# The RWKV-7 core on compact operands: array tiles on the diagonal and 16x16 block inverses

## The chip, the cores and the metric

The kernel runs on one core of a Trainium2 chip. The metric is the device time of one execution in microseconds (us); lower is better. Before the change three timed runs gave 2174.22, 2177.02 and 2177.87 us; the median, 2177.02 us, is the time to predict against. Engines are named as in the profile: PE is TensorE's matmul side, PEld its weight loads, DVE is VectorE, ACT ScalarE, POOL GpSimd, SP the queue that issues the DMAs.

## What is computed

Four layers of a bidirectional sequence model on 256 context and 256 latent tokens of 1024 features, all in fp32: retention, mLSTM, RWKV-7, retention. Only the third layer is touched. Its core is a recurrence over tokens for 16 heads of 64 features in two directions; every head has a state S of 64 x 64:

```
def step(S, inp):
    rt, wt, kt, vt, at, bt = inp
    sa = einsum('bhij,bhj->bhi', S, at)
    S = S * wt[:, :, None, :] + sa[..., None] * bt[:, :, None, :] + vt[..., None] * kt[:, :, None, :]
    return S, einsum('bhij,bhj->bhi', S, rt)
...
mu = y.mean(-1); var = mean(square(y - mu))
o = (y - mu) * rsqrt(var + RWKV_GN_EPS) * gn_g + gn_b
o = (o + bonus) * silu(gate)
```

The scan runs over the context first, then over the latents from the context's last state. `y` is the sum of both directions, normalised head by head.

## The kernel before

Tokens go in 8 chunks of 64 for each direction, heads in 8 pairs (two heads of 64 features fill 128 partitions), pairs in two halves `hf` of four. A unit is one chunk of one direction and one half: four pairs, eight heads. A stage `n` (0 to 7) is four units: two chunks, both directions, one half. Within a chunk the recurrence becomes products: `a`, `r`, `b` and `k` with the decay in them, a strictly triangular 64x64 matrix L of a head, and the inverse of (I - L).

`rk_core` writes the stages out in a fixed order (`ORDER`): `P` (`prep`) loads k, kk and r, makes the decay and the decayed operands; `G` (`grams1`) the products of b with a and r; `H` (`grams2`) those of k; `I` (`solve`) inverts; `J` (`whole`) joins the inverse's parts into M and multiplies the part RB by it to give G; `T` (`step`) of the stage before takes the state one chunk further; `A` is a piece of the last layer's modulation. The framework then orders each engine's queue by its own simulated timeline; every engine works its queue in order.

The operands of both heads of a pair stand block-diagonally in 128x128 tiles, with zeros between (`rb`, `rk`, `rV`, `rR`, `roff`, M, Q, S; zeroed once, then each head's block is written by an operation of its own on 64 partitions). So every product is one full 128-row product for the pair. `bb` (line 1308, VectorE) and `kb` (line 1320, GpSimd) are written that way, S is updated at line 1441, ScalarE copies R (shown as `bdB<-pp`).

`grams1` (line 1330) leaves the 32x32 diagonal blocks of L, 16 pairs in all of a stage, in `AD`, by four copies a unit on ScalarE (`AD<-g`). `solve` masks `AD` (line 1368), transposes it so that a block lies in a partition (line 1369, into `LS`), and eliminates in 30 steps: each is a multiply and an add (lines 1380 and 1381), the first 6 columns on GpSimd in a copy of their own, the rest on VectorE. Lines 1386 and 1387 transpose the result back, as O1 and O2 (`O`). There are two `AD` buffers from the second stage on, and one `LS`. `whole` copies the diagonal blocks of O2 to M (`bdB<-O`, ScalarE), and makes the block below the diagonal with two rounds of products (lines 1398 and 1405); line 1411 gives G. `step` has lines 1426 and 1428 (R), 1435, 1437 and 1438 (the output and the new state in one product of 128 columns). `finish`, once for four steps of a tile, normalises; it takes the square root on ScalarE.

During stage 0, and up to about 1280 us, `rk_rest` runs the projections of r, the values and the gates on TensorE; only then `second()` opens the buffers of the later stages.

Of the kernel before, what the change touches and what calls it, by code (L numbers as in the profile page):

```python
# [7 lines left out]
F32 = mybir.dt.float32  # L8
F32R = mybir.dt.float32r
PSUM = bass.MemoryType.PSUM  # L10
# [19 lines left out]
CS, AKN, GN, WN, RBN, KBN = 8, 8, 4, 4, 5, 2  # L30
ENG = (0, 0, 1, 1, 1, 0, 0, 0)
SC = 6
# [16 lines left out]
class Norm:  # L49
    """The layer's norm of one stream over its features, taken up tile by tile. The sums are of the differences to the  # L50
    mean of the first 128 features, which is within a few standard deviations of the mean."""
# [17 lines left out]
    def add(self, c):  # L69
# [10 lines left out]
        # four partial sums, each on 32 partitions  # L80
# [22 lines left out]
    def finish(self):  # L103
# [16 lines left out]
        # the last layer adds to the latents alone  # L120
# [3 lines left out]
    def late(self):  # L124
        """What the next layer adds to."""
        nc = self.net.nc
        for k in range(KT):
            x = self.x[k]
            nc.gpsimd.tensor_tensor(out=x, in0=x, in1=self.rs, op=OP.mult)
            nc.gpsimd.tensor_scalar(out=x, in0=x, scalar1=self.cs[:, 2, k:k + 1], scalar2=self.cs[:, 3, k:k + 1], op0=OP.mult, op1=OP.add)  # L130


class Net:
# [41 lines left out]
    def filler(self, n=0):  # L175
        """The next piece of what the layer can do at any time."""
# [8 lines left out]
    def open_pw(self, name, bufs=(3, 4, 4), side="right"):  # L185
        """Weights: raw and in their exact parts, on the other side of SBUF."""
# [8 lines left out]
    def open_slots(self, es, name, groups, side="left"):  # L195
        """Slots by what they are for: the tiles of a group take theirs in turn."""
# [3 lines left out]
    def t(self, name, dt=F32, n=512):  # L200
        """A slot of at most 512 columns."""
# [4 lines left out]
    def q(self, name, n=HALF):  # L206
        """A small slot of at most 256 columns."""
# [13 lines left out]
    def pt(self, tag, n=512):  # L221
        """A bank of PSUM."""
# [21 lines left out]
    def unit(self, w, n0, n=256, lo=0, hi=None):  # L244
        """Columns n0.. of w in their exact parts, a pair of [128, n] for each 128 rows."""
# [14 lines left out]
    def proj(self, w, c, lo, hi):  # L260
        """Feature-major product of 128 columns with the tokens lo..hi."""
# [6 lines left out]
    def first_proj(self, jobs, by_k=False, po=4):  # L268
        """proj for a layer's first jobs (w, c, lo): the context's tokens ahead of the latents', or the input's features in turn."""
# [16 lines left out]
    def halves(self, src, h, l, eng=None):  # L286
        """src into its exact parts."""
# [38 lines left out]
    def make_h(self, i, k, st, src, s, b):  # L326
        """h = src * s + b, the input of layer i, in its exact parts (whole for the RWKV layer)."""
# [41 lines left out]
    def out_rows(self, i, w, r0, z, lo0, streams, units=None):  # L369
        """x += gate * (z @ w[r0:r0+512]); z in 4 pairs of tiles of 128 features, from token lo0."""  # L370
# [31 lines left out]
    def log_sigmoid_(self, x, tl):  # L402
        """-(max(-x, 0) + log1p(exp(-|x|))), the logarithm by its atanh series."""
# [22 lines left out]
    def columns(self, ps, parts):  # L426
        """Sums over the partitions of tiles; parts: the columns of 128 of ps that a tile of 128 queries adds to."""
# [3 lines left out]
    def rows(self, col, n, tag="ps"):  # L431
        """Columns of 128 back to n values along the free dimension, the same in every partition."""
# [7 lines left out]
    def rsqrt_rows(self, squares, n, scale, eps, tag="ps"):  # L440
        """(scale * sums over the partitions + eps) ** -0.5 for n columns."""
# [9 lines left out]
    # ---------------------------------------------------------------- retention  # L451
# [37 lines left out]
    def ret_masks(self, h, w384, lg, lgx):  # L489
        """exp(distance * log gamma) summed over the directions, by (query - key): within a stream, latents to context."""  # L490
# [42 lines left out]
    def ret_v(self, h, v, u, w_in):  # L533
        """Half of the values, tokens on partitions."""
# [11 lines left out]
    def ret_values(self, h, qk, v, w_in, w_out, streams, rope, w384, lg, lgx):  # L546
# [4 lines left out]
        # scores of a tile of keys, [keys, queries]  # L551
# [37 lines left out]
        # gates  # L589
# [12 lines left out]
    # ---------------------------------------------------------------- mLSTM  # L602
    def mlstm(self, i, j):
        nc, a = self.nc, self.a
        w_in, w_out = a["ml_w_in"][j], a["ml_w_out"][j]
        with ExitStack() as es:
# [3 lines left out]
            # what goes on into the next layer  # L610
# [12 lines left out]
            def gate_weights(g):  # L623
                """The gates' weights for the convolved and the plain stream, of 4 tiles."""
# [16 lines left out]
            # the convolved stream, that of half the heads by way of memory, and the gates  # L641
# [39 lines left out]
            # the plain stream and the outer gate go by way of memory until their head's turn, as does what the layer adds to  # L681
# [57 lines left out]
    def ml_gates(self, gps, sel, gb, cst):  # L739
        """Rows 32 * direction + head: -G = -max(0, cummax(g)) to memory, g = i - B and exp(-(B + G)) by column."""  # L740
# [76 lines left out]
        # decay of both directions  # L817
# [10 lines left out]
    def ml_scores(self, h, parts, gcol, ecol):  # L828
        """Decayed scores [keys, queries] of both directions and the inverse denominators."""
# [29 lines left out]
        # denominators  # L859
# [29 lines left out]
    def ml_v(self, h, xmd):  # L889
        """Values without their mean over the head, tokens on partitions."""  # L890
# [67 lines left out]
    def spans(jt, d):  # L958
        """The queries that see key tile jt in direction d."""
# [4 lines left out]
    def rwkv(self, i, j):  # L964
        nc, a = self.nc, self.a
        mm = nc.tensor.matmul
        with ExitStack() as es:
# [5 lines left out]
                      ("mrb", (2, 64)), ("mtri", (32,)), ("reset", (512,)))  # L973
# [20 lines left out]
            # by feature, V by token  # L994
# [192 lines left out]
    def rk_core(self, es, e0, K, B, xd, h, xx, p1, p0):  # L1187
# [76 lines left out]
        if ENG[3]:  # L1264
            vcopy = copy
# [417 lines left out]
```

## Time and profile before

| | |
|---|---|
| median of three timed runs | 2177.02 us (2174.22 to 2177.87) |
| profiled execution: span, first to last instruction | 2169.8 us (a time of its own is not listed) |
| TensorE busy | 1958.8 us, 90% |
| VectorE busy | 1351.0 us, 62% |
| ScalarE busy | 942.3 us, 43% |
| GpSimd busy | 614.8 us, 28% |
| core of the RWKV layer | about 1180 to 1760 us of the span |

A busy share is that of the whole span. A product's record covers its way through the array, so that a busy TensorE is not one at its peak. A plain fp32 product stands as two records in the trace, each of them with a weight load. "<-X" in a row means that the time before it ended when X was done.

### The profile page before, as it was taken

To read this page: it belongs to the slowest core of one execution; us is meant where nothing else is said; L and a number is where in the kernel's file an instruction comes from. 1 tells how busy PE (TensorE), PEld (TensorE's weight loads), DVE (VectorE), ACT (ScalarE), POOL (GpSimd) and SP (SyncE) were. 2 spreads that over 40 slices of the span, in tenths; PEclk is the share of its full clock that TensorE was granted. 3 is DMA by queue.
4 is the path that set the end of the run, shared out by engine and by line. 5 is a ranking of instruction groups with operands and counts; after the bars stand their busy time and mean duration, and the time that the engine had idled before them with its cause. 6 is when DMAs were issued, how large, how long until landed. Compare 5 with 4: busy or idle time off the path is not lost.

```text
span 2169.8 us, 35237 instructions
## 1 busy us (share of the span) xinstructions
PE 1958.8 (90%) x13594; PEld 1666.2 (77%) x13594; DVE 1351.0 (62%) x2472; ACT 942.3 (43%) x1853; POOL 614.8 (28%) x940
## 2 busy tenths in 40 slices
PE   6999999998999899987999987778878988999996
PEld 5788888877778777775758976677877776999995
DVE  4463535358536477676857467878877665665554
ACT  3342414134435454333435555555756342444433
POOL 1000000007100334324303266655656332311001
PEclk9999999999999999998899998889889999999998
DMA  9333333333545553441235411111222740233331
GB/s 299 118 98 120 114 112 123 92 107 109 193 155 159 169 175 127 136 155 52 76 132 164 148 57 52 40 28 44 63 60 82 236 148 15 78 113 121 117 98 48
DMA packets 241527, 245.94 MB, mean 113 GB/s; under 512 B 30992, under 2 KB 200080, under 8 KB 241360
## 3 DMA queue, kind: packets, MB, share of 16 engines
q1 hardware_dynamic: 241360, 243.70, 35.6%
q8 instruction: 107, 1.75, 0.3%
q14 instruction: 60, 0.49, 0.1%
HBM read 216.26 MB, written 27.39 MB: 112 GB/s over the span
## 4 chain that ended last, share of the span: by engine, by line
PE 65%; DVE 18%; ACT 5%; DMA 4%; issue 4%; POOL 3%; SPq 0%; DVEq 0%; ACTq 0%; POOLq 0%
PE pp L256 15%; PE pp L257 15%; PE pp L258 15%; DVE LS L1381 2%; DVE sol L1380 2%; PE po L257 2%; PE ps L83 2%; PE po L256 2%; PE po L258 2%; DMA raw<-ada_w 1%; ACT bdB L1200 1%; PE ps L308 1%; DVE wl L240 1%; ACT AD L1200 1%; PE g L1330 1%
## 5 line engine op out<-in xcount | busy, mean ns | idle before, releaser
L240 DVE TENSOR_TENSOR wl<-wraw,wh 128x1024 fp32r<-128x1024 f32 x216 | 270.8, 1255 | 202.9 <-ACT wh L238 195.1
L238 ACT ACTIVATE wh<-wraw 128x1024 fp32r<-128x1024 f32 x216 | 228.6, 1059 | 265.8 <-PE pp L257 111.7
L256 PE MATMUL pp<-hA,wh 128*128 128x512 f32 (+1 forms) x704 | 255.4, 365 | 6.6 <-DVE rp L527 3.0
L257 PE MATMUL pp<-hB,wh 128*128 128x512 f32 (+1 forms) x704 | 254.8, 363 | 0.0
L258 PE MATMUL pp<-hA,wl 128*128 128x512 f32 (+1 forms) x704 | 254.6, 363 | 0.1
L256 PE MATMUL pp<-zh,wh 128*128 128x512 f32 (+1 forms) x620 | 216.0, 351 | 10.6 <-ACT zh L288 6.0
L258 PE MATMUL pp<-zh,wl 128*128 128x512 f32 (+1 forms) x620 | 210.8, 340 | 0.0
L257 PE MATMUL pp<-zl,wh 128*128 128x256 f32 (+1 forms) x512 | 169.2, 330 | 3.1 <-DVE zl L289 3.1
L367 DVE SCALAR_TENSOR_TENSOR x<-pp,mod,x 128x256 f32<-128x256 f32 x192 | 87.3, 480 | 132.8 <-PE pp L258 132.4
L256 PEld LDWEIGHTS pp<-hA,wh 128*128 128x128 f32 x704 | 132.5, 189 | 31.5 <-PE pp L258 3.6
L258 PEld LDWEIGHTS pp<-hA,wl 128*128 128x128 f32 x704 | 133.1, 189 | 23.9 <-issue 1.6
L257 PEld LDWEIGHTS pp<-hB,wh 128*128 128x128 f32 x704 | 133.1, 189 | 22.4 <-issue 1.7
L256 PEld LDWEIGHTS pp<-zh,wh 128*128 128x128 f32 x620 | 117.9, 191 | 40.2 <-issue 10.2
L256 PE MATMUL pp<-wh,hA 128*128 128x256 f32 x512 | 145.7, 286 | 2.0 <-ACT wh L238 1.9
L257 PE MATMUL pp<-wl,hA 128*128 128x256 f32 x512 | 144.9, 284 | 0.8 <-DVE wl L240 0.8
L258 PE MATMUL pp<-wh,hB 128*128 128x256 f32 x512 | 144.5, 283 | 0.0
L258 PEld LDWEIGHTS pp<-zh,wl 128*128 128x128 f32 x620 | 118.3, 191 | 20.2 <-issue 7.6
L1380 POOL TENSOR_TENSOR sol<-AD 128x84 f32<-128x84 f32 (+13 forms) x240 | 97.0, 404 | 117.9 <-ACT AD L1200 100.6
L257 PEld LDWEIGHTS pp<-zl,wh 128*128 128x128 f32 x512 | 98.2, 192 | 16.7 <-issue 5.4
L1381 POOL TENSOR_TENSOR AD<-AD,sol 128x84 f32<-128x84 f32 (+13 forms) x240 | 98.0, 408 | 18.2
L256 PEld LDWEIGHTS pp<-wh,hA 128*128 128x128 f32 x512 | 96.9, 190 | 5.9 <-issue 2.7
L257 PEld LDWEIGHTS pp<-wl,hA 128*128 128x128 f32 x512 | 97.3, 190 | 1.7 <-DVE wl L240 1.0
(519 smaller groups left out, 4911.4 us busy)
## 6 DMA issues: line engine op xcount, KB each, us to landing
wraw<-ret_w_in SPq DMA_DIRECT2D x96, 512.0 KB, 3.7
wraw<-ada_w SPq DMA_DIRECT2D x56, 512.0 KB, 4.0
wraw<-ret_w_out SPq DMA_DIRECT2D x32, 512.0 KB, 3.4
wraw<-ml_w_in SPq DMA_DIRECT2D x32, 512.0 KB, 3.8
wraw<-rk_w_rkvg SPq DMA_DIRECT2D x32, 512.0 KB, 3.6
adaw<-ada_w SPq DMA_DIRECT2D x48, 256.0 KB, 4.5
raw<-ada_w SPq DMA_DIRECT2D x16, 512.0 KB, 7.6
wraw<-ml_w_out SPq DMA_DIRECT2D x16, 512.0 KB, 4.7
```

Of the source, the lines that this page charges most:

```text
L83: nc.tensor.matmul(self.sums[32 * j:32 * j + 32, n * HALF:n * HALF + HALF], net.ones[:, 0:32], src, start=c < 4 and n == 0, stop=c >= 4 an ...
L238: nc.scalar.activation(h, t, ACT.Copy)
L240: (nc.gpsimd if self.nsplit % 4 in self.psplit else nc.vector).tensor_tensor(out=l, in0=t, in1=f(h), op=OP.subtract)
L256: mm(ps, lhs[0], rhs[0], start=start, stop=False)
L257: mm(ps, lhs[0], rhs[1], start=False, stop=False)
L258: mm(ps, lhs[1], rhs[0], start=False, stop=stop)
L308: nc.tensor.matmul(ps[32 * j:32 * j + 32, 0:m].rearrange("p (b q) -> p b q", b=nb), self.csil[:, k, :], raws[k // n][:, k % n, j], start=k ...
L367: self.nc.vector.scalar_tensor_tensor(out=x, in0=ps, scalar=self.gate(i, c, st), in1=x, op0=OP.mult, op1=OP.add)
L1200: copy = lambda o, x: nc.scalar.activation(o, x, ACT.Copy)
L1330: mm(g[:, p, 0:192], cat(u["bb"][:, p]), W[:, p], start=True, stop=True)
L1380: eng.tensor_tensor(out=t, in0=A[:, s + 1:, s:s + 1].broadcast_to([128, m, n]), in1=A[:, s:s + 1, lo:hi].broadcast_to([128, m, n]), op=OP. ...
L1381: eng.tensor_tensor(out=A[:, s + 1:, lo:hi], in0=A[:, s + 1:, lo:hi], in1=t, op=OP.add)
```

## The change

Operands become compact: the two heads of a pair stand one above the other (`[128, 4, 64]` instead of `[128, 4, 2, 64]`), and each head's product is an own small product placed on the array by `tile_position`. A head's 64 rows go to the tile at (0, 0) or (64, 64); the first gram uses four tiles of 64 rows and 32 columns; the products of the inverse's parts use four 32x32 tiles on the diagonal, or two at (0, 32) and (64, 96). Zeroing the buffers falls away but for M and `AD`. `step` makes three sums in PSUM banks of their own (R, the output, the new state) instead of two.

`solve` inverts two 16x16 blocks of each 32x32 block side by side, in 14 steps on VectorE alone; GpSimd has no part in it. The block between them (`Lo`, masked out of the same product) is joined in `whole` by three more rounds of 64 small products each (64, 64 and 64) before the two rounds that were there. The masks go into `grams1` as two VectorE operations a unit.

Other edits: `ENG` moves the `+ 1` of the decay (line 1295) and the bonus product of `finish` (line 1493) from VectorE to GpSimd; R is copied out of PSUM by one ScalarE operation instead of two; the decay of a chunk's end (`Dc`) is one copy instead of two; rings of `b`, `k`, `V` and `R` have four buffers instead of two, M has two; `finish` takes its root with GpSimd's power instead of ScalarE's Sqrt, and loads the values in four DMAs instead of one. Comments and docstrings are emptied, which the cut leaves out.

```diff
-CS, AKN, GN, WN, RBN, KBN = 8, 8, 4, 4, 5, 2
-ENG = (0, 0, 1, 1, 1, 0, 0, 0)
-SC = 6
+CS, AKN, GN, WN, RBN = 8, 8, 4, 4, 5
+ENG = (1, 0, 1, 1, 1, 0, 0, 1)
...
+        pa = self.ph.tile([128, 8, 2, 4, 64], F32, tag="A", name="bdA")
+        pb = self.ph.tile([128, 16, 4, 64], F32, tag="B", name="bdB")
+        rb, rk = [Ring([pa[:, m] for m in ms]) for ms in (range(4), range(4, 8))]
+        rV, rR = [Ring([pb[:, m] for m in ms]) for ms in (range(4), range(4, 8))]
+        rM = Ring([pb[:, m:m + 4].rearrange("p u q t -> p (u q) t") for m in (8, 12)], zero)
...
-            for h in range(2):
-                r = slice(64 * h, 64 * h + 64)
-                E_B.tensor_tensor(out=bb[r, :, :, h].rearrange("p s q t -> p q s t"), in0=st(rev(kk))[r], in1=st(em)[r], op=OP.mult)
+            E_B.tensor_tensor(out=bb.rearrange("p s q t -> p q s t"), in0=st(rev(kk)), in1=st(em), op=OP.mult)
...
         def grams1(u, b0, AD):
             for p in range(4):
-                mm(g[:, p, 0:192], cat(u["bb"][:, p]), W[:, p], start=True, stop=True)
+                for h, r in heads:
+                    for half in range(2):
+                        q = 64 * h + 32 * half
+                        for o, c in (((0, 192), (0, 192)),) if half == 0 else (((0, 32), (32, 64)), ((64, 192), (64, 192))):
+                            mm(g[q:q + 32, p, o[0]:o[1]], bb[r, p, 32 * half:32 * half + 32], W[r, p, c[0]:c[1]], start=True, stop=True,
+                               tile_position=(64 * h, q))
+            for n, t in ((0, AD[:, :, b0:b0 + 4]), (1, u["Lo"])):
+                nc.vector.tensor_tensor(out=t, in0=g[:, :, 0:32].rearrange("p q t -> p t q"), in1=K["m16"][:, n].unsqueeze(2).broadcast_to([128, 32, 4]), op=OP.mult)
-            for q in range(4):
-                r, half = slice(32 * q, 32 * q + 32), q % 2
-                (vcopy if half else copy)(AD[r, :, b0:b0 + 4].rearrange("p t q -> p q t"), g[r, :, 32 * half:32 * half + 32])
...
         def solve(n, AD):
+            for s in range(1, 15):
+                m = 15 - s
+                t = p0.tile([128, 112], F32, tag="sol", bufs=1, name="sol")[:, 0:2 * m * s].rearrange("p (k a b) -> p k a b", k=2, b=s)
+                nc.vector.tensor_tensor(out=t, in0=A[:, :, s + 1:16, s:s + 1].broadcast_to([128, 2, m, s]), in1=A[:, :, s:s + 1, 0:s].broadcast_to([128, 2, m, s]), op=OP.mult)
+                nc.vector.tensor_tensor(out=A[:, :, s + 1:16, 0:s], in0=A[:, :, s + 1:16, 0:s], in1=t, op=OP.add)
...
         def whole(units, O1, O2):
+            for b in range(16):
+                for o, r in quarters:
+                    mm(ps[r, b], units[b // 4]["Lo"][r, :, b % 4], O2[r, :, b], start=True, stop=True, tile_position=(o, o))
+            nc.vector.tensor_tensor(out=Pm, in0=ps, in1=K["m16"][:, 2].unsqueeze(1).broadcast_to([128, 16, 32]), op=OP.add)
+            ...
+                    mm(ps[r, b], O1[r, :, b], Pm[r, b], start=True, stop=True, tile_position=(o, o))
+            for q, (o, r) in enumerate(quarters):
+                (gcopy if q % 2 else copy)(M[r, :, 32 * (q % 2):32 * (q % 2) + 32], ps[r])
+            ...
+                    mm(ps[r, b], Pm[r, b], O1[r, :, b], start=True, stop=True, tile_position=(o, o))
+            copy(MT, ps)
+            ...
+                    mm(ps[r2, b], units[b // 4]["off"][r, b % 4], M[r, b, 0:32], start=True, stop=True, tile_position=(o, o2))
+            for h, (o, r, o2, r2) in enumerate(low):
+                (gcopy if h else copy)(Q[r2], ps[r2])
+            ...
+                    mm(ps[r2, b], MT[r2, b], Q[r2, b], start=True, stop=True, tile_position=(o2, o2))
+            for h, (o, r, o2, r2) in enumerate(low):
+                (gcopy if h else copy)(M[r2, :, 0:32], ps[r2])
...
         def step(u):
+            def sums(*terms):
+                ps = self.pt("pp", 256).rearrange("p (q f) -> p q f", q=4)
+                for n, (x, c, y) in enumerate(terms):
+                    for p in range(4):
+                        for h, r in heads:
+                            mm(ps[r, p], x[r, p, c:c + 64], y[r, p], start=n == 0 and p == 0, stop=n == len(terms) - 1 and p == 3, tile_position=(64 * h, 64 * h))
+                return ps
+            known = lambda c: [(AK, c, V)] + [(W, c, s0)] * (s > 0)
+            copy(R, sums(*known(0)))
+            y_ = sums(*known(64), (G, 0, R))
+            if s < 7:
+                f_ = sums(*known(128), (G, 64, R))
+                nc.vector.tensor_tensor(out=s0, in0=f_, in1=u["Dc"].unsqueeze(2).broadcast_to([128, 4, 64]), op=OP.mult)
```

## Rows read from the trace of the kernel before

**Rows 1.** The page's span line, and TensorE's busy time, share and instructions.
```profile
span 2169.8 us, 35237 instructions
PE 1958.8 (90%) x13594; PEld 1666.2 (77%) x13594; DVE 1351.0 (62%) x2472; ACT 942.3 (43%) x1853; POOL 614.8 (28%) x940
```

**Rows 2.** Windows: stretch, length, busy time of each engine, granted clock, DMA share, GB/s.
```profile
1240.00:1260.00 20.00, 20.00 (x105) 15.99 (x104) 19.03 (x41) 5.75 (x14) 17.06 (x38) 1.00 0.14 46
...
1306.00:1708.00 402.00, 321.29 (x2653) 289.25 (x2653) 321.32 (x657) 222.89 (x539) 252.78 (x508) 0.89 0.24 68
1269.00:1306.00 37.00, 28.86 (x246) 25.87 (x245) 18.29 (x28) 30.96 (x75) 18.42 (x20) 1.00 0.22 65
```

**Rows 3.** The chain that ended last, 1100 to 1860 us: start, duration, what.
```profile
1306.27 1.25 DVE LS L1369
...
1356.73 1.86 DVE O L1387
...
1416.84 1.87 DVE O L1387
...
1658.40 1.91 DVE O L1387
...
1706.11 1.85 DVE O L1387
```

**Rows 4.** Groups by line, 1306 to 1708 us: count, busy us, mean ns, idle before.
```profile
L1380 POOL TENSOR_TENSOR sol<-AD 128x84 f32<-128x84 f32 (+13 forms) x210 | 85.7, 408 | 97.9 <-ACT AD L1200 82.9
L1381 POOL TENSOR_TENSOR AD<-AD,sol 128x84 f32<-128x84 f32 (+13 forms) x210 | 85.3, 406 | 15.8
L1381 DVE TENSOR_TENSOR LS<-LS,sol 128x24 f32<-128x24 f32 (+7 forms) x168 | 68.3, 406 | 7.7 <-ACT AD L1200 3.7
L1380 DVE TENSOR_TENSOR sol<-LS 128x24 f32<-128x24 f32 (+7 forms) x168 | 66.9, 398 | 4.1
...
L1441 DVE TENSOR_TENSOR S<-pp,Dc 64x256 f32<-64x256 f32 x50 | 21.4, 427 | 1.2
...
L1308 DVE TENSOR_TENSOR bdA<-kk,em 64x512 f32<-64x512 f32 x24 | 18.6, 774 | 0.4
...
L1201 DVE COPY G<-ps 128x512 f32<-128x512 f32 x12 | 8.2, 682 | 1.9 <-PE ps L1411 1.9
...
L1380 DVE TENSOR_TENSOR sol<-LS 128x114 f32<-128x114 f32 x14 | 5.8, 411 | 0.2
...
L1380 DVE TENSOR_TENSOR sol<-LS 128x24 f32<-128x24 f32 x14 | 3.6, 259 | 0.3
...
L1358 DVE TENSOR_TENSOR bon<-bon,g 128x128 f32<-128x128 f32 x8 | 2.2, 271 | 0.1
...
L1200 ACT ACTIVATE AD<-g 32x128 f32<-32x128 f32 x96 | 36.7, 382 | 18.6 <-PE g L1330 17.4
L1200 ACT ACTIVATE bdB<-O 32x512 f32<-32x512 f32 x25 | 27.1, 1085 | 9.1 <-DVE O L1387 8.7
```

**Rows 5.** Timeline, TensorE: start, duration, line, output<-inputs, weights, moving operand, count.
```profile
1295.26 1.95 PE L1411 MATMUL ps<-RB,bdB 128*128 128x128 f32 x16
...
1312.14 0.43 PE L1353 MATMUL g<-th,hrk 128*32 128x128 f32 x8
1312.50 1.57 PE L1346 MATMUL g<-W,bdA 128*128 128x192 f32 x8
...
1274.08 2.06 PE L1398 MATMUL ps<-O,q 128*64 128x32 f32 x32
...
1283.98 2.05 PE L1405 MATMUL ps<-Q,AD 128*32 128x64 f32 x32
...
1317.13 0.27 PE L1287 MATMUL g<-tw,cw 64*128 64x128 f32 x1
1317.14 0.27 PE L1287 MATMUL g<-ta,ca 64*128 64x128 f32 x1
1317.24 0.27 PE L1287 MATMUL g<-tw,cw 64*128 64x128 f32 x1
```

More of the change, by code (lines that the diff above doesn't have):

```diff
@@ L1254, in rk_core @@
         rAK = Ring([p1.tile([128, 4, 192], F32, tag="AK", bufs=4, name="AK") for _ in range(4)])
-        S = {}
+        S, lo = {}, [None]
+        heads = [(h, slice(64 * h, 64 * h + 64)) for h in range(2)]
         Y, bon = {}, {}
@@ L1385, in solve @@
+            nc.vector.memset(flat[:, ::33], 1.0)
             O1 = AD
-            nc.vector.transpose(fl(O1), fl(LS))
-            nc.vector.transpose(O2, LS.rearrange("p t s -> p s t"))
+            nc.vector.transpose(fl(O1), flat)
+            nc.vector.transpose(O2, flat.rearrange("p (t s) -> p s t", t=32))
             return O1, O2
         def whole(units, O1, O2):
-            for q in range(4):
-                r, half = slice(32 * q, 32 * q + 32), q % 2
-                (vcopy if half else copy)(M[r, :, q // 2, 32 * half:32 * half + 32], O2[r, :, 0:16].rearrange("p t q -> p q t"))
@@ L1395, in whole @@
[L1395 to L1407 removed]
+            quarters = [(32 * q, slice(32 * q, 32 * q + 32)) for q in range(4)]
@@ new lines, in whole @@
+            copy(MT, ps)
+            ps, Q = wide(), part("Q")
+            low = [(64 * h, slice(64 * h, 64 * h + 32), 64 * h + 32, slice(64 * h + 32, 64 * h + 64)) for h in range(2)]
+            for b in range(16):
+                for o, r, o2, r2 in low:
+                    mm(ps[r2, b], units[b // 4]["off"][r, b % 4], M[r, b, 0:32], start=True, stop=True, tile_position=(o, o2))
+            for h, (o, r, o2, r2) in enumerate(low):
+                (gcopy if h else copy)(Q[r2], ps[r2])
+            ps = wide()
@@ L1486, in finish @@
+            for h, r in heads:
+                for x in range(2):
+                    t0 = 128 * j + 64 * x
+                    nc.sync.dma_start(v[r, x], B["V"][t0:t0 + 64].rearrange("s (p h f) -> s p h f", p=8, h=2)[:, P, h])
             nc.sync.dma_start(sg, B["g"][P, :, tok].rearrange("q p t -> p q t"))
-            bt = bank("ps")[:, 0, 0:8]
-            mm(bt.rearrange("p (q h) -> p q h", h=2), bon[j, hf].rearrange("p s t -> p (s t)"),
-               self.ident.rearrange("p (q c) -> p q c", c=32)[:, :, 0:2], start=True, stop=True)
+            bt = bank("ps")[:, 0, 0:8].rearrange("p (x q) -> p x q", x=2)
@@ L1490, in finish @@
+            for x in range(2):
+                for h, r in heads:
+                    mm(bt[r, x], bon[j, hf][:, x], self.ident.rearrange("p (q c) -> p c q", c=32)[:, h], start=True, stop=True, tile_position=(0, 64 * h))
             bc = tl("bc", 2, 8)
-            copy(bc, bt)
-            v3 = v.rearrange("p q (h j) -> p (q h) j", h=2)
-            E_V.tensor_tensor(out=v3, in0=v3, in1=b3(bc), op=OP.mult)
+            copy(bc.rearrange("p (x q) -> p x q", x=2), bt)
+            E_V.tensor_tensor(out=flat(v), in0=flat(v), in1=b3(bc), op=OP.mult)
@@ L1494, in finish @@
             o, bn = bank("ps"), bank("ps")
-            for p in range(4):
-                mm(o[:, p], Y[j, hf][:, p], self.ident, start=True, stop=True)
-            for p in range(4):
-                mm(bn[:, p], v[:, p], self.ident, start=True, stop=True)
+            for out, src in ((o, Y[j, hf]), (bn, v)):
+                for p in range(4):
+                    for x in range(2):
+                        for h, r in heads:
+                            mm(out[r, p, 64 * x:64 * x + 64], src[r, x, p], K["II"][r], start=True, stop=True, tile_position=(64 * h, 64 * h))
```

138 lines of the change are left out of this document (49 added, 89 removed).

## The prediction

> **What bounds the kernel now.** I read the page first: TensorE is busy for 90% of a span of 2169.8 us [rows 1]. That is an average over four layers, and the change touches only the core of the third, so I went to the windows next. There the core splits in two. Up to about 1280 us the other projections of the layer run on TensorE beside the first stage, and TensorE is busy without a gap (20.00 of 20.00 us in the window from 1240) [rows 2]: what becomes shorter beside it there is hidden. From 1306 to 1708 us no engine is full: of 402 us TensorE is busy for 321, VectorE for 321, GpSimd for 253, ScalarE for 223, and TensorE's granted clock is 0.89 of 2.4 GHz on average, so that it spent part of this stretch at its lower level of 1.2 GHz [rows 2].
>
> The chain of waits tells what sets the pace there. A stage's inversion opens with the transpose at L1369 and closes with the one at L1387. The closings lie at 1356.73, 1416.84 and, later, 1658.40 and 1706.11 us, some 50 to 60 us apart, and the second stage opens at 1306.27 [rows 3]. Seven stages, the second to the eighth, take 1306.3 to 1708.0 us: 57.4 us each. LS, the buffer that is inverted, is one buffer, so inversions follow one another, and one takes nearly a whole period: 30 steps, each two operations on VectorE and two on GpSimd, with all other VectorE work of the stage queued in between. In the groups of lines of these 402 us L1380 and L1381 alone are 135.2 us on VectorE (19.3 a stage) and 171.0 us on GpSimd (24.4 a stage) [rows 4]. So the bound is a serial chain on VectorE and GpSimd, and TensorE waits inside it.
>
> **The change part by part**, a stage at a time (four units, each one chunk of four pairs of heads).
>
> Inversion: 30 steps on 32x32 become 14 steps on two 16x16 blocks at once, 28 operations of 28 to 112 elements, on VectorE alone. Such an operation now takes 259 ns at 24 elements and 411 ns at 114, with GpSimd working beside it [rows 4]. That bounds the 28 at 7.3 and 11.5 us; I take 8.5, nearer to the low end, because GpSimd is out of the step and half of the sizes are under 90. VectorE loses 19.3 and gains 8.5 us; GpSimd loses 24.4 and gains nothing here. The serial piece with its three transposes (4.4 us) becomes about 13 us, a quarter of the period, so it no longer sets the pace.
>
> Masking and copies: ScalarE's copies into AD, 96 of 382 ns in the stretch (up to 16 a stage, 6.1 us), give way to two masked VectorE operations of 128 elements a unit. The nearest row is L1358, 128 elements from PSUM in 271 ns: 8 x 0.27 = 2.2 us. The four copies of O into M, 1085 ns each, leave ScalarE (4.3 us) [rows 4].
>
> Joining on TensorE evicts ten pieces of 512 columns: one sum, four parts of M, MT, two of Q, two of M again; six smaller old copies go. Priced by the 128x512 copy from PSUM at 682 ns [rows 4], VectorE gets five (3.4 us), ScalarE about as much.
>
> Compact operands: the pairs of half-height operations at L1308 (774 ns) and L1441 (427 ns) become one operation of full height, and time goes by columns: two of 774 and 3.5 of 427 ns go from VectorE, 3.0 us [rows 4]. Masking, sums over Y, the step moved to GpSimd (E_L, E_V) and the small old copies take about another 3 us off it; GpSimd has 24 us of new room for that. VectorE, busy for 321 / 7 = 45.9 us a stage now [rows 2], goes to 45.9 - 19.3 + 8.5 + 2.2 + 3.4 - 3.0 - 3 = 35 us. ScalarE and GpSimd fall well below.
>
> TensorE: a product of fp32 is two instructions in the trace. Sixteen of 128 columns (L1411) take 1.95 us, so that they start some 0.11 us apart (the last one lasts 0.3); eight of 192 columns (L1346) 0.16 us apart; of the small ones, 32 with 64 weight columns and 32 moving ones (L1398) take 2.06 us, 32 with 32 and 64 (L1405) 2.05, both some 0.057 to 0.062 apart [rows 5]. Now: 4 units x 40 x 0.11 = 17.6 us in the steps, 5.1 for each kind of gram, 7.4 in joining (2.0 + 1.9 + 3.5), 4.5 for the rest: 39.7. After: tiles on the diagonal go in pairs or fours. That neighbours on different tiles run together is shown: the lora products of L1287 on two row tiles start 10 ns apart, the next pair 0.11 us later, as one product alone would, and the eight of L1353 on four column tiles fit into 0.43 us [rows 5]. Then a step is 32 pairs of two instructions at 0.057 to 0.062: 3.7 to 4.0 us, a stage 14.6 to 16. The first gram, in four 64x32 tiles, keeps the 192 columns of its longest tile and some waits in order: 5.7; the second stays 5.1. Joining has five rounds of 16 blocks, two instructions each at 0.031 (32 columns at half the pace of L1405's 64, or at L1398's) to 0.062: 5 to 10 us, and the last product stays 3.5. With the rest 38 to 45, I take 41.5.
>
> The unknown in joining is how closely small instructions follow. The pairs of L1287 start 10 ns apart, but averaged over a run no row shows less than some 0.05 us an instruction (eight in 0.43 us) [rows 5]. The Trainium skill ("TensorE: Matmul & The Clock Gate", "Wait — 56ns, not 53.3ns?") states that start-to-start never drops below some 25 ns; by that joining's 512 small instructions would take 12.8 us and the stage's TensorE work about 48 us. The 10 ns of L1287's pairs speak against it as a hard floor.
>
> TensorE's busy time now is 321 / 7 = 45.9 us a stage against the 39.7 of dense work; the 6.2 between are fills, waits in a group and the low clock [rows 2]. With the same 6.2 the new stage is 47.7 on TensorE, above VectorE's 35.
>
> **Sum.** The period goes from 57.4 to about 48 us: 7 x 9.4 = 66 us. Before it, in 1269 to 1306, where ScalarE is busy 31 of 37 us [rows 2], 16 AD copies (6.1 us) go: 6 us, from bounds of 0 and 8. After it, the last steps lose 3 us on TensorE (17.6 to 14.6), and joining's longer chain of dependent rounds (five for two, each with an eviction) takes the place of the 4.3 us of O copies: 3 us, from bounds of -3 and 6. Together 75 us. On the span that is 2169.8 - 75 = 2095; the three timed runs have a median of 2177.0, so 7.2 us lie around the span, and the forecast is 2102.
>
> **The rivals.**
> First, TensorE packs better than I allow: its work is 38 us, VectorE's 35, and the stages pipeline with few fills. The period is then 42: 7 x 15.4 + 12 = 120 us, about 2057. For it: TensorE ran at the low clock mainly because it waited for the inversion. Against: two engines at nine tenths, each in order and each feeding the other, seldom come that close.
>
> Second, the dependent rounds and the change of tile shape between groups cost more. Some 35 groups a stage would each start behind the drained previous one; L1353's eight end at 1312.57, so the last began about 1312.30, and the next kind of product begins at 1312.50 [rows 5]: 0.2 us where 0.11 is usual, 0.09 lost. At 0.2 us a group and 12 us of small instructions the stage is 54: 7 x 3.4 + 5 = 29 us, about 2148. The Trainium skill ("TensorEngine Tiling (Array Packing)", "Key Properties") says that changing the mode drains the engine, which agrees with the 0.09.
>
> Third, on the other side: diagonal tiles don't run together. By the code the two row tiles of L1287 write different banks of PSUM, and the column tiles of L1353 share all rows; no row shows two row tiles that write one bank, which is what every product of the change does. If they take turns, the steps are 29 to 32 us a stage, the grams 10 each, joining 23 to 39, the rest 6: at least 80, period 85 to 95, 7 x 33 = 230 us more: about 2400. It decides from the point where serial tiles bring a stage above 57.4 us. "TensorEngine Tiling (Array Packing)", "Gotcha 1: PSUM Pressure", in the Trainium skill says that different row tiles cannot access the same PSUM bank at once; read strictly, that is this rival. For the diagonal, output partitions differ too, as they do in L1353's column tiles, which overlap in one bank; so I hold it unlikely.
>
> Fourth, the change does not bear: TensorE's order, PSUM's two banks for each kind, and GN's four buffers keep the period at 57. About 2175.
>
> **How the numbers follow.** Forecast (period 45 to 52) 0.60; first rival 0.16; second 0.12; third 0.08; fourth 0.04. Faster by over 0.2% (4.4 us, about what a measurement of this kernel can tell from no change) is 0.60 + 0.16 + 0.12 = 0.88, within 0.2% 0.03, slower 0.09. The range is 2045 to 2150: from a little under the first rival to the second.
>
> **What would show it.** Right: inversions of some 13 us with gaps between them, L1387's counterparts 45 to 52 us apart; TensorE busy over 90% of the stretch; pairs on the diagonal starting within 10 ns. Wrong: a pair whose second product starts only when the first is through (third rival); four-tile rounds of 16 blocks over 2.5 us (second); VectorE, not TensorE, full in the windows; or the time from 1280 to 1306 grown by a wait for the first stage.

## The result, and the profile after

The changed kernel takes 2276.62 us (median of 4, 2266.20 to 2279.48) against 2177.03 us before: ratio 1.045, 95% interval 1.0425 to 1.0475. Faster by 75 us was forecast; it is slower by 100 us. The page of after, to be read against [rows 1]:

```profile
span 2277.7 us, 50954 instructions
PE 2031.2 (89%) x21898; PEld 1712.7 (75%) x21898; DVE 1241.5 (55%) x2316; ACT 840.1 (37%) x1653; POOL 424.7 (19%) x432
```

VectorE, ScalarE and GpSimd lost 110, 102 and 190 us of work as intended, and TensorE gained 72 us. In windows (length, busy time of each engine, granted clock, DMA share, GB/s) the six stages from the second to the eighth inversion's start:

```profile
1322.70:1757.80 435.10, 331.56 (x8569) 295.71 (x8567) 215.64 (x462) 139.59 (x376) 91.02 (x72) 0.78 0.18 49
```

No engine is full, as in [rows 2], but now TensorE runs at 0.78 of 2.4 GHz (0.89 before) and still stands idle for 17 us of each stage of 72.5 us. One stage in the chain of waits (start, duration, what; "issue" is time in which the engine waited for nothing that the profile shows), to be read against [rows 3]:

```profile
1389.21 1.15 DVE LS L1370
...
1400.54 1.81 DVE O L1380
...
1402.40 2.26 PE ps L1392 x125
1404.66 2.11 PE pp L1441 x34
1406.76 1.95 PE ps L1397 x120
...
1411.31 1.47 issue
...
1413.10 1.73 PE ps L1409 x64
...
1418.50 1.84 PE ps L1415 x62
...
1427.70 3.73 PE pp L1441 x126
1431.43 1.75 PE g L1284 x26
...
1434.56 1.50 POOL em L1292
...
1436.08 1.24 DVE em L1293
...
1445.87 1.58 DVE bdA L1302
...
1447.49 4.54 PE g L1327 x63
...
1454.43 1.15 DVE LS L1370
```

The inversion (L1370 to L1380) is down to 13.2 us, as forecast. But the rest now follows it in a row: joining rounds (L1392 to L1415) with steps (L1441) between them, steps, the next stage's preparation (L1284 on TensorE, L1292 on GpSimd, L1293 and L1302 on VectorE), its grams (L1327), and only then the next inversion. Before, nearly all that lay in the long inversion's shadow: the next inversion opened 0.5 to 16 us after one had closed, where it now opens 52 to 70 us after. Two openings of before, to be set beside the closings of 1356.73 and 1416.84 in [rows 3]:

```profile
1360.07 1.23 DVE L1369 STREAM_TRANSPOSE LS<-AD 128x1024 f32<-128x1024 f32 x1
...
1419.18 1.24 DVE L1369 STREAM_TRANSPOSE LS<-AD 128x1024 f32<-128x1024 f32 x1
```

The time that TensorE waits in the kernel after, by what ended the wait (us in total, times, longest), the six stages:

```profile
PE g L1327 <- DVE bdA L1302: 21.5, 10, 3.4
PE pp L1441 <- ACT bdB L1199: 21.2, 6, 5.0
PE ps L1392 <- DVE O L1380: 16.5, 6, 3.1
PE g L1347 <- ACT AK L1199: 11.5, 6, 2.0
PE ps L1403 <- issue: 10.9, 6, 2.2
```

Grams wait for the preparation, steps for R's copy, joining for the inversion, once a stage each (the grams up to twice).

### The profile page after: what moved, and what is told of

Its sections match the earlier page's. It is cut to its first block, busy times and chain, and to the rows that moved or that the text cites. A ratio compares the mean times of both kernels' runs of the same rounds, so it can differ in the third digit from the quotient of the medians.

```text
span 2277.7 us, 50954 instructions
## 1 busy us (share of the span) xinstructions
PE 2031.2 (89%) x21898; PEld 1712.7 (75%) x21898; DVE 1241.5 (55%) x2316; ACT 840.1 (37%) x1653; POOL 424.7 (19%) x432
## 4 chain that ended last, share of the span: by engine, by line
PE 71%; DVE 13%; DMA 5%; issue 4%; ACT 4%; POOL 2%; SPq 1%; ACTq 0%; POOLq 0%; DVEq 0%
PE pp L255 14%; PE pp L256 14%; PE pp L257 14%; PE pp L1441 4%; PE po L256 2%; PE po L255 2%; PE po L257 2%; PE g L1327 2%; PE ps L82 2%; PE ps L1422 2%; DMA raw<-ada_w 1%; PE ps L307 1%; DVE sol L1375 1%; DVE wl L239 1%; DVE LS L1376 1%
## 5 line engine op out<-in xcount | busy, mean ns | idle before, releaser
L257 PEld LDWEIGHTS pp<-wh,hB 128*128 128x128 f32 x512 | 98.0, 191 | 0.0
L1441 PE MATMUL pp<-bdB,AK 64*64 64x64 f32 x1472 | 88.2, 251 | 8.5 <-DVE S L1450 5.2
```

The costliest lines, as they stand in the source:

```text
L257: mm(ps, lhs[1], rhs[0], start=False, stop=stop)
L1441: mm(ps[r, p], x[r, p, c:c + 64], y[r, p], start=n == 0 and p == 0, stop=n == len(terms) - 1 and p == 3, tile_position=(64 * h, 64 * h))
```

## Experiments

Ratios are to the kernel before, timed on the same chip. The table gathers the traces: period is the mean of the six stages above; TensorE's busy share and granted clock are those of the same stages (by windows); the last column is how long after an inversion's start the next stage's first Tanh (the head of its preparation) runs, as a mean of six.

| kernel | us | ratio | period | TensorE busy | clock | next preparation after |
|---|---|---|---|---|---|---|
| before | 2177 | 1 | 61.1 | 0.78 | 0.88 | 17 |
| before_14 | 2104.9 | 0.968 | 51.4 | 0.87 | 0.94 | 15 |
| mix | 2143.6 | 0.984 | 54.5 | 0.94 | 0.96 | 13 |
| old_step | 2156.2 | 0.991 | 57.2 | 0.93 | 0.93 | 25 |
| steps_alone | 2245.2 | 1.031 | 72.1 | 0.80 | 0.78 | 39 |
| t_first | 2249.1 | 1.034 | 68.6 | 0.80 | 0.81 | 35 |
| t_p_first | 2250.6 | 1.034 | 69.8 | 0.77 | 0.80 | 30 |
| t_wide | 2245.8 | 1.031 | 69.0 | 0.79 | 0.83 | 43 |
| forced | 2243.8 | 1.031 | 70.0 | 0.77 | 0.78 | 30 |
| old_inv | 2266.2 | 1.042 | 74.9 | 0.70 | 0.76 | 51 |
| warm_steps | 2275.8 | 1.045 | 73.0 | 0.81 | 0.87 | 48 |
| after | 2276.6 | 1.045 | 72.5 | 0.76 | 0.78 | 48 |

The theory at first (Q): the short inversion made the framework lay out the queues so that the next stage stands behind the steps; another order brings the forecast gain. Its rival (C): the compact operands and their chain are dear whatever the order.

### Which part loses

**t_first**, the kernel after with the steps ahead of the inversion in program order:

```diff
-ORDER = "P0 P1 G0 G1 G2 G3 H0 H1 H2 H3 I0 J0 A0 T0-1 T1-1 T2-1 T3-1"
+ORDER = "P0 P1 G0 G1 G2 G3 H0 H1 H2 H3 T0-1 T1-1 T2-1 T3-1 I0 J0 A0"
```

> The changed kernel with one line edited: the stage before's four steps are written out ahead of the inversion and the joining (they stood behind them), so that they get the earlier place in the queues. Theory Q (queues): in the changed kernel the next stage's preparation stands on TensorE behind this stage's joining and most of its steps, so that preparation, first gram, inversion and joining are one serial chain of 65 to 83 us a stage; with the steps moved under the inversion the period falls to 50 to 58 us and the time to 2130 to 2190 us. Theory C (cost): the tile products themselves and TensorE's lower clock make the stage long; then the order changes little and the time stays above 2250 us.

Measured 2249.14 us, 1.0341 [1.0319, 1.0363]: 27 us of 100. **t_p_first** also takes the next stage's preparation ahead of joining:

```diff
+ORDER = "G0 G1 G2 G3 H0 H1 H2 H3 T0-1 T1-1 T2-1 T3-1 I0 P0+1 P1+1 J0 A0"
```

> As the run with the steps ahead of the inversion, and the next stage's preparation is written out ahead of this stage's joining as well. Theory Q: the preparation (some 14 us from its lora products to the operands of the first gram) leaves the chain; period 45 to 55 us, 2110 to 2180 us, no slower than with the steps alone moved. Theory C: above 2250 us.

Measured 2250.59 us, 1.0342 [1.0319, 1.0364]. Neither comes near the range of Q: program order alone is worth a quarter of the loss, and Q in this form fell.

**old_inv**, the kernel after with the inversion of before (30 steps on VectorE and GpSimd) and without the three new rounds (`whole` takes the blocks from O2 and O1):

> The changed kernel with the inversion of before put back: 30 steps on 32x32 blocks shared by VectorE and GpSimd, the block inverse copied straight into M, and none of the three new rounds of small products. All other products stay on diagonal tiles. Theory Q: the chain has a long inversion (some 32 us for 11) and a joining shorter by 8 to 12 us, the steps lie under the inversion: 2230 to 2300 us. Theory C: with 384 small instructions fewer on TensorE a stage, faster than the changed kernel by over 40 us, below 2235 us.

Measured 2266.18 us, 1.042 [1.0394, 1.0447]. With 384 small instructions a stage fewer and the long inversion back (31 us in its trace), the time is nearly that of after. This lies in the range of Q, and C's (below 2235 us) is missed; it also shows that the loss doesn't hang on the short inversion. **before_14**, the kernel before with fewer eliminations:

```diff
-            for s in range(1, 31):
+            for s in range(1, 15):
```

> The kernel before with 14 of the 30 elimination steps (the other 16 are left out), all else as it was: what a short inversion alone is worth in the old layout and its order. If the inversion sets the period there, as the prediction says: 16 steps of 2 x 0.4 us and what stands between them, some 10 to 16 us a stage, 70 to 110 us in all: 2067 to 2107 us. If a short inversion by itself turns the order into a serial chain (a form of Q), within 30 us of the 2177 us of before.

Measured 2104.9 us, 0.9679 [0.9656, 0.9702]. The 16 eliminations left out are not replaced by anything here. So the first reading held: the inversion set the pace in the old layout, and a short one is worth 70 us there. **mix** makes that a full kernel: block-diagonal operands, grams and steps of before; `solve` and `whole` of after. The masks are taken once a stage in `solve`, and Q shares the buffer of Pm:

```diff
+            for x in range(2):
+                L = rLo.next()
+                nc.vector.tensor_tensor(out=L, in0=AD[:, :, 8 * x:8 * x + 8], in1=K["m16"][:, 1].unsqueeze(2).broadcast_to([128, 32, 8]), op=OP.mult)
...
-            nc.vector.tensor_tensor(out=o, in0=o, in1=K["mtri"].unsqueeze(2).broadcast_to([128, 32, 16]), op=OP.mult)
+            nc.vector.tensor_tensor(out=o, in0=o, in1=K["m16"][:, 0].unsqueeze(2).broadcast_to([128, 32, 16]), op=OP.mult)
```

> One part alone: the kernel before with its block-diagonal operands and its full-size products for grams and steps, and only the inversion of the change (14 elimination steps on 16x16 blocks, three joining rounds of 32x32 tiles, the two lower rounds as tiles). If the compact operands carry the loss (theory M, to which old_inv at 1.042 and before_14 at 0.968 point), it takes what before_14 took, 2105 us, plus what three rounds of some 2 us and their copies add to a stage where they are not covered, 0 to 8 us over 7 stages: 2105 to 2165 us, faster than before. If the joining rounds are the loss wherever they stand (changes of tile shape, TensorE's lower clock behind them), it is above 2190 us.

Measured 2143.61 us, 0.9844 [0.983, 0.9859]: faster than both before and after. Its six stages in windows, and a piece of its chain:

```profile
1316.70:1643.80 327.10, 306.46 (x5231) 275.67 (x5230) 240.73 (x487) 195.00 (x505) 81.00 (x76) 0.96 0.22 64
```
```profile
1373.70 0.42 DVE S L1457
...
1377.91 0.20 DVE LS L1381
...
1379.31 1.89 DVE O L1385
...
1381.24 2.23 PE ps L1397 x122
...
1414.70 1.16 DVE LS L1375
```

TensorE is busy for 306 of 327 us at 0.96 of its clock, with the same tile rounds. State updates (L1457) run within the inversion, and the next one opens 33.5 us after the first round. From the second inversion's start to the last one's end a stage takes 49.3 us (forecast: 48). **old_step** undoes the steps alone, with the finishing that belongs to their layout:

```diff
-            copy(R, sums(*known(0)))
-            y_ = sums(*known(64), (G, 0, R))
...
+                mm(f_[0:m, p], AK[:, p, 64:64 + m], cat(V[:, p]), start=True, stop=False)
+                if s:
+                    mm(f_[0:m, p], W[:, p, 64:64 + m], cat(s0[:, p]), start=False, stop=False)
+                mm(f_[0:m, p], G[:, p, 0:m], cat(R[:, p]), start=False, stop=True)
```

> One part undone: the kernel after with the steps (state, values, R, their sums and the finishing) in the block-diagonal form of before; grams, inversion and rounds stay compact. If the steps in 64x64 tiles carry the loss (three sums of 16, 24 and 24 products in place of two of 8 and 12), the time falls to 2170 to 2225 us. If the loss lies in the grams, in the order of the work or in the joining rounds, it stays at 2250 to 2290 us.

Measured 2156.23 us, 0.9907 [0.9892, 0.9922]. One part gives back 120 us, more than the whole loss and more than expected. Its windows and its longest waits of TensorE:

```profile
1317.60:1660.80 343.20, 319.46 (x6358) 270.25 (x6358) 219.68 (x488) 151.43 (x401) 98.25 (x84) 0.93 0.22 61
```
```profile
PE g L1348 <- ACT AK L1199: 5.7, 3, 2.9
PE ps L1404 <- issue: 5.5, 5, 1.7
PE pp L1450 <- ACT bdB L1199: 3.1, 4, 1.5
```

**steps_alone** is mix with the compact steps (and their finishing and their two moves to GpSimd), grams as before:

> The kernel mix (full-size block-diagonal grams of before, inversion of the change; 0.984) with the compact steps of the change: the steps' part alone on top of it. old_step (0.991) showed that undoing the steps gives back 120 of the change's 100 us. If the compact steps are dear by themselves, 2230 to 2275 us here too. If they are dear only beside compact grams, 2140 to 2190 us.

Measured 2245.17 us, 1.0312 [1.0283, 1.034]: 102 us over mix. The steps are dear by themselves. The compact grams with their masks make up the rest: 31 us between steps_alone and after, 13 us between mix and old_step.

**old_fin** tells the steps from the finishing: the kernel after with the finishing of before.

> The kernel after with the finishing of before alone (the output rows of two chunks stacked in 128 partitions: 8 full-size transposes and one load in place of 32 products of 64 columns each for y and v and four loads); the steps keep their 64x64 tiles and three sums, and y is written by two instructions in place of one. Two of the six periods of after last 83 us, those around finishings, against 65 to 70. If the finishing is what makes the steps' part dear, the long periods go: 2185 to 2235 us. If it is the sums, 2255 to 2285 us.

Measured 2270.25 us, 1.045 [1.0431, 1.047]. It is the steps, not the finishing.

### Why the steps lose

TensorE's time for the steps does not tell: summed from each record's start to the next's, or to its own end where a pause follows, it is some 21.5 us a stage in after and in old_step alike. Of the 15.3 us by which a stage is longer in after, 13.3 are idle time of TensorE (17.3 us against 4.0) and 2.0 are busy time, at a clock of 0.78 against 0.93. Each of the next runs tries one candidate.

**one_bank**: output and state in one bank of PSUM, products with known operands first, so that a step takes two banks as before.

```diff
-            y_ = sums(*known(64), (G, 0, R))
...
+                y_, f_ = sums(2, *known(64, 0), *known(128, 1), (G, 0, R, 0), (G, 64, R, 1))
```

> The kernel after with the output's and the state's sum of a step in one bank of PSUM, the products that need only known operands (32) ahead of those that need R (16): two banks taken per step, as in before, in place of three, out of the same two. In the kernel after TensorE waits 80 us in the stretch 1389 to 1758 us, 22 us of it in the steps for the copy of R and the state. If the three sums in two banks and their order are what makes the compact steps dear (theory B), most of these 22 us and the waits of the work queued behind go: 2190 to 2245 us. If it is the mere number of small products, TensorE's clock or the order of the queue, 2260 to 2285 us.

Measured 2268.99 us, 1.0427 [1.0402, 1.0452]. With the order of t_first (**one_bank_t**):

> The same with the steps ahead of the inversion in program order, as in t_first (1.034). If banks and queue order add up (theory B), 2150 to 2215 us; if the banks don't count, 2235 to 2260 us, as t_first.

Measured 2258.43 us, 1.0379 [1.0355, 1.0402]. Banks are not it.

**f_first** writes the state's sum and update ahead of the output's sum (which then reads the state already updated).

> The kernel after with the state's sum and update written ahead of the output's sum in each step, so that the 24 products of y no longer stand between R and the state. If the steps' serial chain is what sets the period (24 products, 0.66 us at 2.4 GHz and 1.3 at 1.2 GHz, twice in a stage), 2255 to 2270 us; if not, 2272 to 2282 us.

Measured 2272.79 us, 1.0439 [1.0418, 1.046]. The output's sum also has to wait for the update here, so this says little.

**warm** adds a dense product ahead of four joining rounds, **warm_steps** one ahead of each output's sum as well:

```diff
+                if warm:
+                    mm(t, self.ident, K["a2"][:, 0:512], start=True, stop=True)
```

> The kernel after with one added product of 128 rows, 128 columns of weights and 512 columns, its result overwritten, ahead of each of the last four joining rounds of a stage: 4 x 0.85 us of work at 2.4 GHz, 27 us more over 8 stages. If TensorE's lower clock (0.70 to 0.84 granted between 1300 and 1850 us) is what makes its chain long and the pauses between the small rounds bring it, the mean granted clock of that stretch rises above 0.87 and the time falls to 2200 to 2262 us. If the clock follows the small tiles themselves or is not what counts, the time is 2275 to 2310 us.

> The kernel after with dense products in TensorE's pauses: the one ahead of four joining rounds as in warm (which raised the clock from 0.77 to 0.85 and took 13 us off), and one of 256 columns (0.43 us at 2.4 GHz) ahead of the sum of y in every step, where TensorE waits for R. If the lower clock carries most of the loss, the granted clock of 1300 to 1700 us rises above 0.92 and the time falls to 2190 to 2245 us. If the pauses themselves carry it, 2255 to 2290 us.

Measured 2263.97 us, 1.0408 [1.039, 1.0425], between the two expectations, and 2275.76 us, 1.0446 [1.0426, 1.0465]. Windows of warm_steps:

```profile
1312.50:1750.80 438.30, 356.27 (x8684) 288.69 (x8682) 214.01 (x462) 139.65 (x376) 90.94 (x72) 0.87 0.18 48
```

The clock rose from 0.78 to 0.87 and the period stayed at 73 us. The added products (some 7.5 us a stage) stand in the same queue, and what the clock gives back can be hidden behind them; so what the lower clock is worth is not shown.

**t_wide**: half as many products of twice the columns.

```diff
-                            mm(ps[r, p], x[r, p, c:c + 64], y[r, p], ...
+                            mm(ps[r, p:p + 2], x[r, p, c:c + 64], y[r, p:p + 2], ...
```

> The kernel after with half as many products in the steps, each of 128 columns in place of 64 (of every second pair of heads the operand is left out and its neighbour's stands in): TensorE streams as many columns, with 32 products in place of 64 per step. If the number of small products is what makes the steps dear (their issue, and a queue laid out for so many), 2165 to 2235 us. If the columns, the waits between the sums or TensorE's clock are, 2255 to 2285 us.

Measured 2245.78 us, 1.0309 [1.0288, 1.0329], between the two expectations. TensorE's time for the steps is near that of after (some 20 us a stage), and the next stage's preparation comes 4 us earlier. Halving the number of products is worth 31 of the 100 us; what a still smaller number would give was not tried.

**r_dve** (R copied on VectorE) and **eng_old** (the two moves to GpSimd undone) each take away a wait that the trace names:

> The kernel after with R copied on VectorE in place of ScalarE. In after TensorE waits 18.6 us in 5 stages (up to 5.0 us) for this copy, which stands in ScalarE's queue behind the next stage's exponentials, and these wait for GpSimd and VectorE. If this crossing in ScalarE's queue is a main part of the loss, 2225 to 2255 us; if the wait only moves to VectorE's queue or elsewhere, 2262 to 2290 us.

> The kernel after with the two operations that the change moves to GpSimd back on VectorE (the addition at the head of the next stage's preparation, 1.49 us on GpSimd, for which VectorE waits 41 us in 11 places, and the scaling of the values in the finishing, 1.04 us). If these two lie on the chain that sets the period (twice 1.1 us a stage and some of the waiting behind), 2240 to 2262 us; if other waits take their place, 2266 to 2285 us.

Measured 2270.98 us, 1.0432 [1.0407, 1.0457], and 2266.46 us, 1.0427 [1.0412, 1.0443]. The waits go elsewhere: in r_dve the steps wait 14.9 us, in four waits from 1385 to 1720 us, for the copy in VectorE's queue.

**forced** takes the program order of t_p_first and writes out the order of the queues in three places besides, same instructions.

```diff
+            with behind(last["T"] if n > 1 else None):
+                u = prep(d, n // 2 * 2, n % 2)
...
+            with behind(last_p[0] if 0 < n < 7 else last["T"] if n else None):
+                whole(U[n], *O[n])
...
+                if s == SPLIT:
+                    es_q = behind(first_s)
```

> The kernel after, the same instructions, with the order of the queues written out in three places (order alone, no wait for an end): the inversion's elimination steps from the sixth on stand behind the first two state updates of the stage before on VectorE, the next stage's first products behind the last step on TensorE, and the joining rounds behind these. If the loss is that steps, next stage and inversion stand in each other's way in the queues (in after, the state updates come 16 to 43 us after an inversion's start and in mix and old_step some within it, and the next stage's preparation starts at 44 us against 17 us), the period falls from 72 us to below 64 and the time to 2150 to 2215 us. If the loss lies in the compact steps themselves, 2235 to 2265 us, as with the program order alone (t_p_first, 2251).

Measured 2243.82 us, 1.0311 [1.0294, 1.0328]: 7 us less than t_p_first, with the period (70.0 and 69.8 us) and the place of the preparation (30 us) as they were there. In the six stages 70% of the steps' products are now issued within an inversion (10% in after, 19% in t_p_first) and 16 of 24 state updates (5 and 0), and with these in it the inversion takes 20 to 22 us for 13. TensorE's waits in 1380 to 1720 us:

```profile
PE ps L1409 <- DVE Pm L1405: 19.2, 5, 4.6
PE pp L1454 <- DVE S L1463: 13.0, 4, 4.2
PE ps L1421 <- DVE bdB L1204: 12.3, 5, 3.4
```

The first round's result (Pm) is late, as in t_p_first (26.2 us in six stages), because on VectorE it stands behind the scan of the next stage's preparation. One wait has taken another's place.

**mix_t**, the order of t_first on mix, shows the same from the other side:

> The kernel mix (products of before, inversion of the change; 0.984) with the steps ahead of the inversion in program order. TensorE is busy for 45 to 48 of each 50 us between 1300 and 1650 us in mix, so an order has at most 3 of 50 us to give: 2125 to 2150 us. If the order matters as much as between the kernel after and t_first (27 us), 2105 to 2122 us.

Measured 2174.81 us, 0.9997 [0.9984, 1.0011]: the order that took 27 us off after puts 31 us on mix. Both expectations were wrong.

**What stays open.** That the compact steps carry the loss is shown twice (old_step, steps_alone), and that TensorE stands idle for it. Why the rest fits so badly round them is not settled. In the table the kernels whose next preparation runs some 25 us or less after an inversion's start have periods under 62 us, those at 30 us and later more than 68 us; that is a correlation. As a cause it would explain little: t_first, one_bank_t, t_p_first and forced bring the preparation from 48 us to between 36 and 30, and the period falls by 2 to 4 us. Nor does the period go by where the steps stand: within an inversion lie 70% of their products in forced (70.0 us) and 32% in old_step (57.2 us). No run puts the preparation ahead of the compact steps, to the 13 to 17 us of mix and before; that test is missing.

## Why the prediction was wrong

- **What bounds before**: right. before_14 takes 70 us off by shortening the inversion alone.
- **Inversion**: right. 13.2 us for 13; the 28 operations take 6.8 us for 8.5 (row below, 242 ns each; the low bound was 7.3).

```profile
L1376 DVE TENSOR_TENSOR LS<-LS,sol 128x28 f32<-128x28 f32 (+6 forms) x84 | 20.3, 242 | 2.2
L1375 DVE TENSOR_TENSOR sol<-LS 128x28 f32<-128x28 f32 (+6 forms) x84 | 20.3, 242 | 2.7
L1293 DVE TENSOR_TENSOR_SCAN em<-creset,em 128x512 f32<-128x512 f32 x12 | 16.8, 1397 | 33.5 <-POOL em L1292 33.5
```

- **VectorE 35 us a stage**: right, 215.64 / 6 = 35.9. But a share says nothing of waits: the move of `+ 1` to GpSimd, costed at nothing because GpSimd has room, puts 1.5 us ahead of VectorE's scan, which waits 33.5 us for it in six stages (last row); undone alone, with the other move, it is worth 10 us at most (eng_old).
- **Joining, 5 to 10 us**: 9.9 us by starts, at the upper end, and mix bears it at a gain. The floor of 25 ns for the 512 small instructions, cited there from the Trainium skill ("TensorE: Matmul & The Clock Gate", "Wait — 56ns, not 53.3ns?"), does not agree with the 14 ns measured (last section).
- **Grams, 5.7 and 5.1 us**: the pace was right (16 records of 192 columns start within 1.2 us at 2.4 GHz), but a stage shows 8.3 and 5.7 us: two thirds of the first gram's time lies at 1.2 GHz.
- **Steps, 14.6 to 16 us**: the pace was right (29 ns a record at 2.4 GHz, by the first window of the last section; 14 to 15 us for a stage's some 500 records); a stage shows 21.3 us, nearly half of it at 1.2 GHz.
- **"The same 6.2" of fills and low clock**: this is the step that failed. The sum let TensorE's busy time set the period and priced its waits at nothing, as if its queue would be full once VectorE's was short; yet before the change it already waited 13 us a stage (61.1 us, 47.9 of them busy). TensorE's busy time is 55.3 us a stage for 47.7, and 17 us of waiting come on top. The shorter inversion did not bring these waits: behind one of 16 to 20 us mix waits 3.4 us a stage and takes 49.3, near the forecast, and with a long one back (31 us) old_inv takes 69.0. The compact steps brought them, which the sum priced by the pace of their products alone. Against the sum: the start, before the second inversion, came 16 us later (forecast 6 earlier); the seven stages from its start to the last inversion's end take 64.1 us each in place of 57.4 (forecast 48), 47 us; from there to the end 507 us in place of 462 (forecast 3 less), 45 us. These 45 lie in the core too: its last product comes 107 us after the last inversion in place of 60, and the layer behind it takes 400 us in both.
- **Rivals**: the third (diagonal tiles take turns) is refuted. Sixteen records of 192 columns on two 64x64 tiles that write one bank (row below, at 2.4 GHz) take as long as the eight full ones of L1346 in [rows 5]. Read strictly, "Gotcha 1: PSUM Pressure" of the Trainium skill ("TensorEngine Tiling (Array Packing)") does not agree with this. The second rival priced the dependent rounds and put the stage at 54 us, still 3.4 us shorter; mix has the same rounds in a stage of 49.3, so they are not what costs. The fourth named the queue's order as a reason for "no change" at 0.04; it should have been the rival on the other side, as one mechanism: joining, steps, preparation and grams, which overlapped before, laid out one behind the other.

```profile
1330.75 1.52 PE L1347 MATMUL g<-W,bdA 64*64 64x192 f32 x16 [2.02 <-ACT AK L1199]
```

## What to carry to other kernels

Products that are given a new form are not priced by their array time alone: the compact steps take as much of TensorE's time as the old ones (some 21.5 us a stage), and cost over 100 us, mostly by the waits around them. When a sum lets one engine's busy time set the period, add up beside it the chain as if nothing overlapped: here joining, steps, preparation and grams are 52 us in a row on four in-order queues (1402 to 1454 us), which with the inversion is the whole new stage shown. The truth lies between the two, and only a run tells where: mix, with an inversion nearly as short, comes out near the sum. Engine shares, even right ones, bound a period only from below. Try the two halves of such a change apart: here one is worth 33 us by itself (mix), and the other, the compact operands, costs 133 on top of it (after against mix).

## What the hardware showed

Windows of t_first (columns as above): steps, a second joining round at either level of the clock, a fourth round, and the stretch around it.

```profile
1397.00:1405.10 8.10, 8.10 (x280) 8.10 (x276) 0.85 (x2) 1.54 (x4) 0.00 (x0) 0.99 0.16 36
...
1408.60:1410.40 1.80, 1.80 (x127) 1.80 (x128) 0.00 (x0) 1.80 (x8) 0.13 (x1) 1.00 0.94 263
1574.34:1576.14 1.80, 1.80 (x126) 1.80 (x128) 1.74 (x3) 0.75 (x2) 1.03 (x2) 0.50 0.34 100
...
1418.98:1420.66 1.68, 1.68 (x65) 1.68 (x64) 0.00 (x0) 1.62 (x7) 1.60 (x2) 0.50 0.57 171
...
1423.00:1428.00 5.00, 5.00 (x108) 4.40 (x108) 4.94 (x9) 2.75 (x7) 0.19 (x1) 0.50 0.03 9
1435.00:1441.00 6.00, 6.00 (x150) 4.71 (x149) 2.92 (x8) 1.94 (x6) 0.00 (x0) 1.00 0.01 3
```

The fourth round in mix:

```profile
1349.26:1350.27 1.01, 1.01 (x63) 1.01 (x64) 1.00 (x2) 0.98 (x4) 0.07 (x1) 1.00 0.00 0
```

- A round of four 32x32 tiles takes 1.80 us for its 128 records, 14 ns each, at 2.4 GHz (1408.60) and at 1.2 GHz (1574.34) alike: its pace does not go by TensorE's clock. Rounds on two tiles do follow the clock: 26 ns a record at 1.2 GHz (1418.98), 16 ns at 2.4 GHz (64 in 1.01 us in mix, last row).
- After a pause of 2.2 us within the third round (up to 1412.94) the clock fell to 0.50, and it was still there in 1423 to 1428 us although TensorE was busy without a gap; it was back at 1.00 from 1435 us, among the last joining products and the grams. In mix, with the same rounds between full-size products, the mean is 0.96.
- In nearly every kernel with the new rounds TensorE pauses, mostly 1 to 3 us, in the third one for nothing that the profile shows (10.9 us in six stages in the waits of after). In warm and warm_steps, where a dense product stands ahead of this round, such pauses there come to 1.4 and 0.8 us. Why was not tried.
